# Layer 1's modulations of x summed on VectorE and GpSimd during the products with w_out

## The chip, the cores and the metric

The kernel runs on one core of a Trainium2 chip. The engines work side by side, each through its own queue of instructions in a fixed order: TensorE (PE in the profile, with its weight loads as PEld) multiplies matrices into PSUM, VectorE (DVE), ScalarE (ACT) and GpSimd (POOL) work element by element, and SyncE (SP) issues most of the DMAs between HBM and SBUF. The metric is the time of one execution on the device in microseconds (us), as the median of several runs. Lower is better.

## The reference

A diffusion transformer of two layers, with 512 image tokens (x) and 256 context tokens (ctx), width 1024. Each layer first makes modulations out of a conditioning vector: one product with w_ada (1024 x 6144) gives six vectors of 1024 values, for x from c and for ctx from c_ctx.

```python
def adaln(cond, w_ada, b_ada):
    m = jax.nn.silu(cond) @ w_ada + b_ada
    return jnp.split(m, 6, axis=-1)
...
    for l in range(DEPTH):
        update_ctx = l < DEPTH - 1
        sh1, sc1, gt1, sh2, sc2, gt2 = [m[:, None, :] for m in adaln(c, w_ada[l], b_ada[l])]
        csh1, csc1, cgt1, csh2, csc2, cgt2 = adaln(c_ctx, w_ada[l], b_ada[l])
        h = rms_norm(x, g_mix[l]) * (1 + sc1) + sh1
        hc = rms_norm(ctx, g_mix[l]) * (1 + csc1) + csh1
        ...
        x = x + gt1 * (o @ w_out[l])
        x = x + gt2 * swiglu(rms_norm(x, g_ffn[l]) * (1 + sc2) + sh2, w_gate[l], w_up[l], w_down[l])
        if update_ctx:
            ...
    return rms_norm(x, g_final)
```

Between the two lies a mixer: six heads of global attention, a Fourier mix and six heads of attention in a window. In layer 1 ctx is not updated any more, so that there only sh1 and sc1 of ctx are needed, and of the chunks 2 to 5 (gt1, sh2, sc2, gt2) only those of x.

## The kernel before

All data is kept transposed: 1024 channels as eight blocks of 128 partitions, the tokens along the free dimension. Most products are made in three matmuls from operands split into a high and a low part (`mm3`, L90; `split`, L103: ScalarE rounds the high part, VectorE subtracts for the low one).

The modulations come in three groups of two chunks each (`adaln`, L251). A step loads one block of 128 rows and 2048 columns of w_ada (1 MB, on SP, into one of the two `raw` staging buffers) and multiplies it on TensorE by a stationary block of 32 columns of `ct`, in which two columns hold silu(c) and silu(c_ctx): four matmuls side by side in four column strips of the array (L278). In the attention VectorE adds the result to a sum in SBUF (L290). After eight steps `last` transposes the sum back (L296), adds the bias (L301) and makes the scale with the norm's gain (`mod`, L313). So c and ctx are served at once.

Layer 0's group 0 is made at the start. All else is made in the second half of each layer's attention (the six window heads), as fill: `mix` (L1056) gives each piece of filling work a cost, and `attention` (L970) hands out pieces after each finished unit (two query blocks of one head, 12 units in layer 1) in proportion to the units done. The list `ada` has groups 1 and 2 of the layer itself and, in layer 0, group 0 of layer 1; it is interleaved with the steps of the Fourier mix. A step of `ada` costs 2.5, of `fb` (Fourier inputs) 5, of the Fourier mix 1.3.

`w_out` (L1165) then loads x back (`xt`, L1173), and goes through the eight output blocks d, two to a load (`load_pair`, L142, 1 MB, in `raw`). `one` makes the product of a block for a range of tokens in one of three PSUM banks (`mm`), and VectorE adds it to x (L1182); ScalarE squares it for the next norm (L411), VectorE sums the squares (L415). The first four blocks are made for all tokens (x: `XR`, then ctx: `CR`), the last four (`late`) first for x, so that its norm can begin (`stat`, L425 and L426, matmuls against a column of ones; `rstd`, L339 on GpSimd; L441), and only then for ctx. In layer 1 there is no ctx, and x is done in two halves. The norm's results (L1212 to L1222) feed the first product of the feed-forward part (`first`, L1362), while `tokens` (L1261) makes sums of token blocks into the tiles th0 to th3 and tl0 to tl3. `spare` (L1235) lends these same tiles for other uses before and after that time.

The order on each engine is not simply that of the code: a planner lays the instructions out by the readiness that it expects and by their place in the code, and adds the waits. The queue of an engine, SP's among them, is then in order: an instruction that waits holds up all behind it.

Of the kernel before, what the change touches and what calls it, by code (L numbers as in the profile page):

```python
# [11 lines left out]
AF = mybir.ActivationFunctionType  # L12
ALU = mybir.AluOpType
# [4 lines left out]
P = 128  # L18
D = 1024
KB = D // P  # L20
# [26 lines left out]
class Builder:  # L47
# [68 lines left out]
    def raw(self):  # L116
        return self.wp.tile([P, 2048], F32, name=self.nm("raw"), tag="raw", bufs=2)
# [133 lines left out]
    def adaln(self, l, g, raw, psum, tile, hold=KB, js=range(4)):  # L251


        nc = self.nc
        n = len(js)
        dj = js[1] - js[0]
        jv = slice(js[0], js[-1] + 1, dj)
        w = self.a["w_ada"][l].rearrange("k (g j c) -> k g j c", j=4, c=512)[:, g, jv]
        st = {}

        by = 4 // n
        e = 32 * n * by

        def step(k0):


            if k0 % hold == 0:
                st["ps"] = psum()
            rs = []
            for k in range(k0, k0 + by):  # L270
                rs.append(raw()[:, 0 : n * 512].rearrange("p (j c) -> p j c", c=512))
                self.queue(rs[-1], w[k * P : (k + 1) * P])
            end = None
            for i in reversed(range(by)):
                with self.tc.issue_after(end) if end else ExitStack():
                    for j in range(n):
                        o = 32 * (n * i + j)
                        end = nc.tensor.matmul(  # L278
                            st["ps"][o : o + 32, :],
                            self.ct[:, k0 + i, :],  # L280
                            rs[i][:, j],
                            start=(k0 % hold == 0),
                            stop=((k0 + by) % hold == 0),
                            tile_position=(0, o),
                        ).ins
            if k0 + by == hold:
                st["sb"] = tile()[0:e, 0:512]
                nc.scalar.copy(st["sb"], st["ps"][0:e])
            elif (k0 + by) % hold == 0:
                nc.vector.tensor_add(st["sb"], st["sb"], st["ps"][0:e])  # L290

        def last():
            sb = st["sb"]
            pt = psum() if hold < KB else st["ps"]
            for cb in range(4):
                nc.tensor.transpose(pt[:, cb * e : (cb + 1) * e], sb[:, cb * P : (cb + 1) * P], self.ident[0:e, 0:e])  # L296
            gj = lambda v: v.rearrange("p (g j c) s -> p g j c s", g=3, c=4)[:, g, jv]
            src = pt[:, 0 : 4 * e].rearrange("p (c i j s) -> p i j c s", c=4, i=by, s=32)[:, :, :, :, 0:2]
            b = gj(self.bada[l].unsqueeze(2)).to_broadcast([P, n, 4, 2])
            for i in range(by):  # L300
                nc.vector.tensor_tensor(gj(self.ada[l]), src[:, i], gj(self.ada[l]) if i else b, op=ALU.add)  # L301
            for i in range(2):
                ks = [4 * (4 * g + j - (24 * i + 8) // 4) for j in js]
                ks = [k for k in ks if 0 <= k < KB]
                if ks:
                    self.mod(l, i, slice(ks[0], ks[-1] + 4))

        return [lambda k=k: step(k) for k in range(0, KB, by)] + [last]

    def mod(self, l, i, r):  # L310
        g = (self.gmix if i == 0 else self.gffn)[l][:, r]
        sc = self.ada[l][:, 24 * i + 8 : 24 * i + 16, :][:, r]
        self.nc.vector.scalar_tensor_tensor(  # L313
            self.smod[l][i][:, r], sc, 1.0, g.unsqueeze(2).to_broadcast([P, r.stop - r.start, 2]), op0=ALU.add, op1=ALU.mult
        )
# [740 lines left out]
    def mix(self, l, hi, lo, ws, outs):  # L1056
        nc = self.nc
        full = l < DEPTH - 1
        self.qkv_tiles(full)
        krs, rms, turn = self.qkv_a(l, hi, lo, ws, outs)  # L1060
# [33 lines left out]
        for f in va:  # L1094
# [3 lines left out]
        mods = lambda m, g: cost(  # L1098
            2.5, self.adaln(m, g, self.raw, self.fl, lambda: self.f2([P, 512], "sb"), 1)
        )  # L1100
# [3 lines left out]
            for c, tb in ((kc, 3), (qc, 2)):  # L1104
                c[0] = (0, lambda f=c[0][1], tb=tb: self.late(f, tb))
        fill = kc[0:3] + qc[0:1] + kc[3:] + qc[1:]
        ada = mods(l, 1) + mods(l, 2)
        if full:
            ada += mods(l + 1, 0)

        held = []

# [52 lines left out]
    def w_out(self, l, oh, ol):  # L1165

        nc = self.nc
        full = l < DEPTH - 1
        w = self.a["w_out"][l]
# [4 lines left out]
        acc = self.fp.tile([P, T], F32, name=self.nm("acc"), tag="acc", bufs=1)  # L1174
        hs = [self.utile(F32) for k in range(KB)]

        def one(d, wt, rng, s):
            r0, r1 = rng
            ps = self.mm()[:, 0 : r1 - r0]
            wh, wl = wt  # L1180
            self.mm3(ps, [(wh[:, k], wl[:, k], oh[k][:, r0:r1], ol[k][:, r0:r1]) for k in range(KB)])
            nc.vector.scalar_tensor_tensor(  # L1182
                xt[d][:, r0:r1], ps, self.gt(l, 0, d, s), xt[d][:, r0:r1], op0=ALU.mult, op1=ALU.add
            )
            self.stat_add(acc, xt[d], rng, d)

        rngs = (XR,) if full else XH
        late = []
        for dp in range(KB // 2):
            rv = self.load_pair(w[:, dp * 256 : (dp + 1) * 256])  # L1190
            for j in range(2):
                d = 2 * dp + j
                wt = self.pair_half(rv, j)
                if d >= KB - LATE:
                    late.append((d, wt))
                    continue
                one(d, wt, XR, 0)
                if full:
                    one(d, wt, CR, 1)
        bcs = []  # L1200
        for rng, bank in zip(rngs, (self.fl, self.mm)):
            for d, wt in late:
                one(d, wt, rng, 0)
            bcs.append(self.stat_bc(acc, rng, bank()))
        hi, lo = self.act
        n = (T if full else SX) // 2
        last = []
# [24 lines left out]
                self.norm_raw(hs[k], xt[k], bc, CR, l, k, 1)  # L1232
        return xt, hs

    def spare(self, i):  # L1235

        tag = ("th", "tl")[i // 4] + str(i % 4)
        t = self.fp.tile([P, 3, T // 2], F32, name=self.nm("sp"), tag=tag, bufs=1)
        return t.rearrange("p a b -> p (a b)")[:, 0:512]

    def utile(self, dt):
        return self.fp.tile([P, T], dt, name=self.nm("u"), tag="u", bufs=8)
# [642 lines left out]
```

## Time and profile before

| | |
|---|---|
| time of three runs | 1558.27 us median (1555.56 to 1558.91) |
| profiled execution | 1555.41 us, of it 1553.6 us of span |
| mean granted TensorE clock | 0.99 |
| VectorE, ScalarE, GpSimd busy | 73%, 49%, 36% of the span |
| loads of w_ada | 40 of 1 MB in the attention of both layers, 16 of 512 KB at the start |

The span is the time from the first to the last instruction. In the profile a line L278 is line 278 of the kernel before; a helper's line stands for all who call it, so groups are told apart by tiles (`fl<-raw,ct` is a matmul into PSUM tile fl from raw and ct). A number behind x is a count of instructions, then come the busy time, the mean duration in ns and the idle time of the engine just before, with what ended it.

### The profile page before, as it was taken

The numbers are of one execution on the slowest core, as the hardware profiler recorded it, in microseconds if no ns is written. First come the engines' busy times: TensorE is split into PE (matmuls) and PEld (weight loads), VectorE is DVE, ScalarE is ACT, GpSimd is POOL, SyncE is SP. The second block draws the span as 40 slices with busy tenths as digits, with TensorE's granted clock in tenths as the row PEclk, the third lists the DMA queues.
The fourth block names the chain that finished last, engine by engine and source line by source line (L and its number), as shares of the span: only waits on it lengthen the run. The fifth ranks groups of instructions, "written<-read, shape, count | busy, mean of one in ns | idle before, by whom it ended". The sixth has DMA issues, their size and how long they took to land.

```text
span 1553.6 us, 25611 instructions
## 1 busy us (share of the span) xinstructions
PE 1485.4 (96%) x9769; PEld 1363.6 (88%) x9769; DVE 1133.1 (73%) x1907; ACT 763.9 (49%) x1542; POOL 556.7 (36%) x463
## 2 busy tenths in 40 slices
PE   6989989999999999999999998999999999999997
PEld 3789967688999999999899978987799898988987
DVE  3767577753978878876887866667749778777775
ACT  3556566642744444444435545666637344444344
POOL 0354345310256656452000025353401444344432
PEclk9999999999999999999999999999999999999999
DMA  9510085851133543446883541065441423223221
GB/s 339 197 48 29 1 263 159 290 190 29 54 130 130 163 138 123 161 137 227 307 301 110 167 128 35 28 201 189 141 134 52 136 82 109 83 82 126 92 82 55
DMA packets 124298, 211.59 MB, mean 136 GB/s; under 512 B 6456, under 2 KB 87120, under 8 KB 119056
## 3 DMA queue, kind: packets, MB, share of 16 engines
q1 hardware_dynamic: 116320, 203.92, 38.2%
q0 software_dynamic: 7856, 6.04, 2.0%
q8 instruction: 77, 1.26, 0.3%
q14 instruction: 45, 0.37, 0.1%
HBM read 180.96 MB, written 28.97 MB: 135 GB/s over the span
## 4 chain that ended last, share of the span: by engine, by line
PE 69%; DVE 10%; DMA 8%; ACT 4%; POOL 4%; issue 4%; SPq 1%; POOLq 0%; DVEq 0%; ACTq 0%
PE mm L90 15%; PE lg L90 14%; PE fl L90 13%; DVE w L103 5%; PE mm L1506 4%; PE mm L945 4%; PE lg L1506 4%; PE mm L937 2%; ACT w L103 2%; PE fl L278 2%; DMA raw<-in_w_up_dram 2%; PE lg L833 2%; PE lg L841 2%; DMA ra<-in_w_ada_dram 2%; PE fl L1506 1%
## 5 line engine op out<-in xcount | busy, mean ns | idle before, releaser
L103 DVE TENSOR_TENSOR w<-raw,w 128x512 fp32r<-128x512 f32 (+1 forms) x336 | 314.7, 949 | 113.5 <-ACT w L103 108.1
L103 ACT CAST w<-raw 128x512 fp32r<-128x512 f32 (+1 forms) x336 | 228.5, 701 | 316.4 <-POOL raw L1324 94.1
L90 PE MATMUL lg<-ahi,w 128*128 128x384 f32 (+1 forms) x640 | 151.2, 312 | 6.9 <-DVE w L103 3.1
L90 PE MATMUL fl<-ahi,w 128*128 128x384 f32 (+1 forms) x640 | 153.5, 308 | 0.9 <-ACT acc L1385 0.9
L852 POOL TENSOR_TENSOR p<-p,rc 128x768 f32<-128x768 f32 (+2 forms) x84 | 111.4, 1344 | 116.9 <-DVE rc L850 105.3
L90 PE MATMUL lg<-th,w 128*128 128x384 f32 (+1 forms) x640 | 150.4, 311 | 1.4 <-DVE u L1448 1.2
L90 PE MATMUL mm<-u,w 128*128 128x512 f32 (+1 forms) x576 | 137.9, 378 | 3.9 <-DVE u L103 2.2
L339 POOL TENSOR_TENSOR rs<-ms,mhalf 128x8 f32<-128x8 f32 (+3 forms) x22 | 28.6, 1304 | 288.7 <-DVE ms L335 288.7
L90 PEld LDWEIGHTS lg<-ahi,w 128*128 128x128 f32 x640 | 111.5, 191 | 11.2 <-ACT w L103 5.1
L90 PE MATMUL fl<-w,ahi 128*128 128x256 f32 x576 | 115.0, 293 | 5.9 <-DVE w L103 3.8
L90 PEld LDWEIGHTS mm<-u,w 128*128 128x128 f32 x576 | 98.0, 190 | 20.9 <-DVE u L103 3.5
L90 PEld LDWEIGHTS lg<-th,w 128*128 128x128 f32 x640 | 111.7, 191 | 3.3 <-DVE u L1448 1.5
L90 PEld LDWEIGHTS fl<-ahi,w 128*128 128x128 f32 x640 | 112.0, 190 | 2.5 <-ACT acc L1385 1.1
L90 PE MATMUL mm<-ahi,w 128*128 128x256 f32 (+1 forms) x448 | 107.1, 330 | 0.0
L1324 POOL TENSOR_TENSOR raw<-raw 128x512 f32<-128x512 f32 x40 | 62.3, 1559 | 110.8 <-DVE w L103 110.8
L90 PEld LDWEIGHTS fl<-w,ahi 128*128 128x128 f32 x576 | 93.5, 196 | 8.0 <-DVE w L103 4.3
L103 DVE TENSOR_TENSOR t<-mm,t 128x512 fp32r<-128x512 f32 x108 | 74.0, 687 | 34.7 <-ACT t L103 34.0
L90 PE MATMUL lg<-tl,w 128*128 128x384 f32 (+1 forms) x320 | 99.3, 310 | 0.0
L90 PE MATMUL lg<-alo,w 128*128 128x384 f32 (+1 forms) x320 | 99.2, 310 | 0.0
L1316 POOL TENSOR_TENSOR s<-raw 128x512 f32<-128x512 f32 x40 | 54.6, 1366 | 123.3 <-DMA raw<-in_w_up_dram 75.8
L90 PE MATMUL fl<-alo,w 128*128 128x384 f32 (+1 forms) x320 | 98.7, 308 | 0.0
L844 DVE TENSOR_REDUCE neg<-lg 128x1 f32<-128x768 f32 (+2 forms) x96 | 80.7, 851 | 19.9 <-PE lg L841 19.0
(367 smaller groups left out, 3980.7 us busy)
## 6 DMA issues: line engine op xcount, KB each, us to landing
raw<-in_w_ada_dram SPq DMA_DIRECT2D x40, 1024.0 KB, 4.9
raw<-in_w_gate_dram SPq DMA_DIRECT2D x22, 1024.0 KB, 5.2
raw<-in_w_up_dram SPq DMA_DIRECT2D x22, 1024.0 KB, 5.3
uh<-uh SPq DMA_DIRECT2D x33, 384.0 KB, 4.8
w<-uh SPq DMA_DIRECT2D x33, 384.0 KB, 4.6
wd<-in_w_down_dram SPq DMA_DIRECT2D x47, 256.0 KB, 5.1
raw<-in_w_in_dram SPq DMA_DIRECT2D x11, 1024.0 KB, 5.5
raw<-in_w_down_dram SPq DMA_DIRECT2D x11, 1024.0 KB, 4.8
```

The lines of the kernel that those rows point to most:

```text
L90: mm = lambda a, b, **k: self.nc.tensor.matmul(out, a, b, skip_group_check=more, **k)
L103: return self.nc.scalar.copy(hi, src).ins, self.nc.vector.tensor_sub(lo, src, hi).ins
L278: end = nc.tensor.matmul(st["ps"][o : o + 32, :], self.ct[:, k0 + i, :], rs[i][:, j], start=(k0 % hold == 0), stop=((k0 + by) % hold == 0) ...
L833: nc.tensor.matmul(o, qt[:, qs], K1[:, kv, k0 : k0 + w], start=True, stop=False)
L841: nc.tensor.matmul(o, qt[:, qs], K2[:, kv, k0 : k0 + w], start=False, stop=True)
L844: nc.vector.tensor_reduce(ng, lv, axis=AX.X, op=ALU.max, negate=True)
L852: nc.gpsimd.tensor_tensor(pt, pt, rc[:, i : i + 1].to_broadcast(list(pt.shape)), op=ALU.mult)
L937: nc.tensor.transpose(ps[:, col + j * P : col + (j + 1) * P], pt[:, c : c + P], self.ident)
L945: nc.tensor.matmul(out[:, r], V[:, kb, kv, :], t[:, c], start=first and n == 0, stop=end and n == len(todo) - 1,)
L1316: nc.gpsimd.tensor_add(s1, a21, a22)
L1324: nc.gpsimd.tensor_sub(a12, a12, a11)
L1506: nc.tensor.matmul(ps, w[:, x, c], u[:, y], start=(not more and k == 0 and j == 0), stop=(k == npc - 1 and j == 2), skip_group_check=True,)
```

## The change

Layer 1's groups 1 and 2 are not made in its attention any more: its list `ada` is empty, and layer 0's is as before. A new function `matvec` makes one chunk of 1024 values for x alone. A step loads 128 rows of w_ada and the chunk's 1024 columns (512 KB), and multiplies each row with its value of silu(c), a scalar for each partition, while adding it to a sum of 128 x 1024 in SBUF. The first step of a chunk writes the sum on ScalarE. The others are one instruction of VectorE, or, for a chunk with `pooled` set, a scaling on ScalarE and an addition on GpSimd. `last` adds up the 128 partitions: eight matmuls with a 128x128 block of the sum as the stationary operand and the column of ones as the moving one, into one bank; VectorE adds the bias and, for chunk 4, makes the scale.

Layer 0's `w_out` makes chunks 2 and 3 of layer 1 (VectorE; they share four buffers, and have one sum each) and chunk 4 (`pooled`, one buffer and one sum). Layer 1's `w_out` makes chunk 5 of its own (VectorE, the same four buffers). The buffers and sums are the tiles that `spare` lends, which now hands out 1024 columns where asked. The steps stand in the code after the products of `w_out`: after each call of `one` for the first four blocks, and for the late ones of x, `more` hands out a share of them, 27 in ten calls in layer 0 (every third one of chunk 4) and 9 in six calls in layer 1.

```diff
+    def matvec(self, l, i, room, acc, pooled):
+        nc = self.nc
+        w = self.a["w_ada"][l][:, i * D : (i + 1) * D]
+        st = {}
+
+        def step(k):
+            r = room()
+            nc.sync.dma_start(r, w[k * P : (k + 1) * P])
+            c = self.ct[:, k, 0:1]
+            if k == 0:
+                st["acc"] = acc()
+                nc.scalar.activation(st["acc"], r, AF.Identity, scale=c)
+            elif pooled:
+                nc.scalar.activation(r, r, AF.Identity, scale=c)
+                nc.gpsimd.tensor_add(st["acc"], st["acc"], r)
+            else:
+                nc.vector.scalar_tensor_tensor(st["acc"], r, c, st["acc"], op0=ALU.mult, op1=ALU.add)
+
+        def last():
+            ps = self.lg1()[:, 0:KB]
+            for k in range(KB):
+                nc.tensor.matmul(ps[:, k : k + 1], st["acc"][:, k * P : (k + 1) * P], self.ones, start=True, stop=True)
+            r = slice(i * KB, (i + 1) * KB)
+            a = self.ada[l][:, r, 0]
+            nc.vector.tensor_tensor(a, ps, self.bada[l][:, r], op=ALU.add)
+            if i == 4:
+                nc.vector.scalar_tensor_tensor(self.smod[l][1][:, :, 0], a, 1.0, self.gffn[l], op0=ALU.add, op1=ALU.mult)
+
+        return [lambda k=k: step(k) for k in range(KB)] + [last]
...
-        ada = mods(l, 1) + mods(l, 2)
-        if full:
-            ada += mods(l + 1, 0)
+        ada = mods(l, 1) + mods(l, 2) + mods(l + 1, 0) if full else []
...
+        turn = [0, 4, 1, 5]
+
+        def room():
+            i = turn.pop(0)
+            turn.append(i)
+            return self.spare(i, 1024)
+
+        if full:
+            one3 = self.matvec(l + 1, 2, room, lambda: self.spare(2, 1024), False)
+            two3 = self.matvec(l + 1, 3, room, lambda: self.spare(3, 1024), False)
+            own = self.matvec(l + 1, 4, lambda: self.spare(6, 1024), lambda: self.spare(7, 1024), True)
+            mods = []
+            for i, f in enumerate(one3 + two3):
+                mods.append(f)
+                if i % 2:
+                    mods.append(own.pop(0))
+            every = len(mods) / 10
+        else:
+            mods = self.matvec(l, 5, room, lambda: self.spare(2, 1024), False)
+            every = len(mods) / 6
+        made = [-every]
+
+        def more():
+            made[0] += every
+            while mods and made[0] > 0.5:
+                made[0] -= 1
+                mods.pop(0)()
+
         for dp in range(KB // 2):
...
                 one(d, wt, XR, 0)
+                more()
                 if full:
                     one(d, wt, CR, 1)
+                    more()
         bcs = []
         for rng, bank in zip(rngs, (self.fl, self.mm)):
             for d, wt in late:
                 one(d, wt, rng, 0)
+                more()
             bcs.append(self.stat_bc(acc, rng, bank()))
...
-    def spare(self, i):
+    def spare(self, i, w=512):
...
-        return t.rearrange("p a b -> p (a b)")[:, 0:512]
+        return t.rearrange("p a b -> p (a b)")[:, 0:w]
```

## The prediction

> **What bounds the kernel now.** I read the page first: busy time and share of the span of each engine.
>
> ```profile
> PE 1485.4 (96%) x9769; PEld 1363.6 (88%) x9769; DVE 1133.1 (73%) x1907; ACT 763.9 (49%) x1542; POOL 556.7 (36%) x463
> ```
>
> TensorE is busy for 96% of the span. That is an average, so next comes the view of busy time by stretches, over the places that the change touches: layer 0's w_out (337 to 395), the start of its feed-forward part (395 to 432), the second half of layer 1's attention (1027 to 1130), and layer 1's w_out (1130 to 1165).
>
> ```profile
> core 0: us, PE busy (x) PEld busy (x) DVE busy (x) ACT busy (x) POOL busy (x), PEclk, DMA share, GB/s
> 337.00:385.00 48.00, 48.00 (x267) 41.98 (x266) 18.10 (x26) 10.92 (x17) 0.00 (x0) 1.00 0.28 97
> 385.00:395.00 10.00, 10.00 (x88) 10.00 (x87) 6.80 (x11) 4.53 (x8) 1.03 (x1) 1.00 0.34 107
> 395.00:432.00 37.00, 36.67 (x219) 36.59 (x218) 36.88 (x70) 27.81 (x58) 8.01 (x6) 1.00 0.09 29
> 1027.00:1060.00 33.00, 31.34 (x243) 23.04 (x243) 25.57 (x42) 20.17 (x41) 14.72 (x13) 1.00 0.79 271
> 1060.00:1102.00 42.00, 42.00 (x333) 34.91 (x335) 32.22 (x62) 27.05 (x65) 17.97 (x16) 1.00 0.46 164
> 1102.00:1130.00 28.00, 24.66 (x156) 19.97 (x150) 18.68 (x33) 15.75 (x35) 9.05 (x7) 0.94 0.49 167
> 1130.00:1165.00 35.00, 35.00 (x230) 32.16 (x229) 16.53 (x26) 10.98 (x17) 3.44 (x2) 1.00 0.34 110
> ```
>
> Columns: the stretch, its length, each engine's busy time (instructions). TensorE is the bound in every one of them. In layer 0's w_out VectorE has 29.9 us free of 48, ScalarE 37, and GpSimd did nothing. From 395 to 432 VectorE is as full as TensorE (36.88 and 36.67 of 37): no room there. From 1102 to 1130, the tail of layer 1's attention, TensorE is idle for 3.3 us.
>
> **What is removed.** Layer 1's two lists of modulation steps (groups 1 and 2) leave its attention. The groups of lines have their matmuls (between 1027 and 1107) and their additions on VectorE (all lists); below them three pieces of the chain in order of time (start, length, what).
>
> ```profile
> L278 PE MATMUL fl<-raw,ct 128*32 128x512 f32 x128 | 18.1, 604 | 1.3 <-issue 1.0 <-DMA raw<-in_w_ada_dram 0.2
> ...
> L290 DVE TENSOR_TENSOR sb<-sb,fl 128x512 f32<-128x512 f32 x35 | 23.9, 683 | 9.2 <-PE fl L278 8.8
> ```
>
> ```profile
> 1037.97 1.00 PE fl L278 x8
> ...
> 1059.89 0.44 PE fl L296 x4
> ...
> 1102.97 5.18 DMA raw<-in_w_out_dram
> ```
>
> 128 records in eights are 16 steps. The busy 18.1 us count ends that overlap with other matmuls; on the chain a step takes 1.00 us, so 16.0 in all. The four transposes that close a list take 0.44 us, for two lists 0.9. TensorE's waits in front of the steps, 1.0 + 0.2 = 1.2 us, go too. Together **-18.1 us**, if TensorE stays the bound. What is late next: between 1027 and 1102 TensorE is left with 73.3 - 15 x 1.00 = 58 us of work, VectorE with 57.8 less some 13 additions of 0.68, so 49, ScalarE with 46. TensorE still leads, by 18%.
>
> The fill between the heads is dealt out by cost. Without the steps (18 at a cost of 2.5) its total falls from 68 to 23, so the rest of the fill comes later and closer: the first Fourier step after about half of the heads instead of after two of twelve. Its work is the same and still ends with the last head; I cost that at nothing, between -1 (fewer clashes) and +3 (the idle time that TensorE shows in the tail, again).
>
> The sixteen loads of 1 MB go as well. They hold the two staging buffers that w_out's weights need (the third row above). The last step releases the buffer, and then 5.2 us pass until w_out's first weights land, with their splits in the attention's tail on ScalarE and VectorE. The load will now be issued early. The gain lies between 0 and the 3.3 us that TensorE idles there; the other waiters of that tail (softmax and its splits) stay, so I take a bit under half, **-1.5 us**.
>
> **What is added.** Four vectors (chunks 2, 3, 4 in layer 0's w_out, chunk 5 in layer 1's) of eight loads of 512 KB and one closing step each. The closing step has eight matmuls against a column of ones. The same form, stationary 128x128 with one moving column, stands in the norm's sums:
>
> ```profile
> 385.62 0.36 PE L425 MATMUL mm<-ones,acc 128*128 128x1 f32 x2
> ...
> 386.73 0.36 PE L426 MATMUL mm<-ones,sq 128*128 128x1 f32 x2
> ```
>
> Five of those pairs take 386.73 - 385.62 = 1.11 us, 0.222 each. 4 x 8 x 0.222 = 7.1 us on TensorE, in stretches without a gap: **+7.1 us** (5.3 in layer 0, 1.8 in layer 1).
>
> The products of weights and vector have the nearest rows in the groups of lines by shape:
>
> ```profile
> L103 DVE TENSOR_TENSOR w<-raw,w 128x1024 fp32r<-128x1024 f32 x64 | 81.6, 1278 | 16.7 <-ACT w L103 11.7 <-PE lg L90 3.5 <-DMA xt<-xsc 0.5
> ...
> L103 ACT CAST w<-raw 128x1024 fp32r<-128x1024 f32 x64 | 67.0, 1052 | 43.0 <-PE mm L90 25.7 <-PE lg L90 10.3 <-DMA raw<-in_w_in_dram 2.8
> ...
> L711 POOL TENSOR_TENSOR qcx<-t,t 128x512 f32<-128x512 f32 x4 | 5.2, 1294 | 12.8 <-DVE t L710 12.8
> ```
>
> VectorE takes 1.28 us for 128x1024 with two inputs, ScalarE 1.05, GpSimd 2.6 (twice its half). In layer 0, VectorE has 14 such products, 18 us in 29.9 free ones; ScalarE 10, 10.5 us in 37; GpSimd 7, 18.2 us, where it was idle. TensorE waits for VectorE only when the three product banks are full, and today VectorE waits for TensorE:
>
> ```profile
> 376.18 0.75 DVE L1182 SCALAR_TENSOR_TENSOR xt<-mm,ada,xt 128x512 f32<-128x512 f32 x1 [2.90 <-PE mm L90]
> ```
>
> So these lie beside other work, as long as they end before 395. Whether they do is set by their loads and by the chain on GpSimd:
>
> ```profile
> GB/s 339 197 48 29 1 263 159 290 190 29 54 130 130 163 138 123 161 137 227 307 301 110 167 128 35 28 201 189 141 134 52 136 82 109 83 82 126 92 82 55
> ...
> ra<-in_w_ada_dram SPq DMA_DIRECT2D x16, 512.0 KB, 9.7
> ...
> raw<-in_w_in_dram SPq DMA_DIRECT2D x4, 512.0 KB, 5.0
> ```
>
> ```profile
> 331.59 5.76 SPq L1173 DMA_DIRECT2D xt<-xsc  x8
> ```
>
> ```profile
> 420.28 0.54 DVE L103 TENSOR_TENSOR tl<-u,th 128x384 fp32r<-128x384 f32 x1
> ```
>
> The loads queue on SP behind x (issued until 337.4). 24 of them are 12.6 MB; with 2 MB of w_gate and w_up, at the 339 GB/s of the busiest slice, 43 us: until about 380. The two vectors on VectorE have four buffers and end by then. Chunk 4 has one buffer, so its load, scaling and addition follow one another: with the 5.0 us landing 8 x 5.0 + 8 x 1.05 + 7 x 2.6 = 67 us, so 404; with five loads in flight 5 x 0.52 MB / 339 GB/s = 7.7 us (the 9.7 of the first rows is such a burst), for all eight 88 us, so 425. The first steps are crowded and the last ones alone: I take 414. Its buffers are wanted back by the first tl splits at about 420, and chunk 4 itself only in layer 1, so being late costs nothing by itself. Behind each waiting load on SP stand w_gate and w_up, which the feed-forward part needs shortly before 395; they wait for one load at a time, so some 10 us, and have twice that. If that cover went, each microsecond would be one on TensorE.
>
> Two things are not hidden. GpSimd's short instruction for the norm's root, on the way to the feed-forward part, can stand behind one 2.6 us addition. And two engines can stop each other, as the timelines of GpSimd and VectorE show:
>
> ```profile
> 399.31 1.60 POOL L1317 TENSOR_TENSOR raw<-raw 128x512 f32<-128x512 f32 x1
> ```
>
> ```profile
> 396.21 0.61 DVE L1217 SCALAR_TENSOR_TENSOR alo<-u,ada,ahi 128x384 fp32r<-128x384 f32 x1
> ...
> 399.70 1.62 DVE L1217 SCALAR_TENSOR_TENSOR alo<-u,ada,ahi 128x384 fp32r<-128x384 f32 x1
> ```
>
> A VectorE instruction that takes 0.61 us alone took 1.62 beside a GpSimd addition, ending 0.41 us after it. Two or three additions fall after 395, where VectorE is full. For both, and for TensorE meeting the ones matmuls a little early, I take **+3.0 us**, one addition with its hand-over; the ends are 0 and the second rival's 16. In layer 1's w_out seven products of 1.28 us on VectorE (16.5 of 35 busy) and no GpSimd addition: nothing.
>
> Sum: -18.1 - 1.5 + 7.1 + 3.0 = **-9.5 us**. The profiled execution took 1555.4 us, 1553.6 of span and 1.8 around it, so 1545.9; the median of the runs is 2.9 above it: **1549 us**.
>
> The Trainium skill (SBUF — State Buffer, "SBUF: two separate sides") speaks against the change: it states that VectorE with two SBUF inputs and GpSimd take one pair of ports as an exclusive lock for a whole instruction. The 1.62 us row agrees with it. By that rule all seven additions could stop VectorE, and the sum would be the third rival's or worse; without it, mine or the last rival's.
>
> **The rivals.**
> - *Attention doesn't shrink in full* (0.12). Without the fill, the path from logits over VectorE, ScalarE and GpSimd back to TensorE could set the pace. For it: VectorE would be at 49 of 58 us, and the tail shows such idle time. Against: from 1060 to 1102 TensorE has no gap. At half of 18.1: -0.4, 1558.
> - *TensorE held by GpSimd's chain* (0.14), the other side. TensorE works in a fixed order, and chunk 4's ones matmuls stand where the planner thinks them ready; behind them stand w_out's last products. The chain is 8 links long, so an error in each adds up. Placed at 404 and ready at 420, between the two ends: 16 us instead of my 3, so +3.5, 1562. It decides from a wait of some 12 us on. In code order, behind the third of the late tiles (the L1182 row at 376.18), even the 404 would mean a wait of 27, so 1573. Against: the order is not that of the code, since the first product of w_out runs ahead of attention's last ones,
>
> ```profile
> 324.96 0.50 PE L90 MATMUL mm<-ahi,w 128*128 128x512 f32 x1
> ...
> 329.98 0.39 PE L945 MATMUL mm<-t,Vc 128*128 128x256 f32 x2
> ```
>
> and waits for planned loads are small (0.2 us in the 16 steps above).
> - *VectorE stopped by GpSimd* (0.14). Three additions after 395 stop a full VectorE for 3 x 2.6 = 7.8 us, and TensorE follows: -4.7, 1553.
> - *Better* (0.10): no stall, the tail's idle time gone: -18.1 - 3.3 + 7.1 = -14.3, 1544.
>
> My own case has 0.50. About 0.2% (3.1 us) can be told from no change. Faster by more: 0.50 + 0.14 + 0.10 = 0.74; within: the first rival, 0.12; slower: 0.14. The range runs from 1541 to 1560: it takes in all but the GpSimd chain's own cases and some hundredths below.
>
> **What would show it.** Right: in layer 1's attention no L278 and L296, and the time from its second half's start to w_out's is some 19 us shorter with TensorE still full; the new ones matmuls in pairs at 0.22 us; VectorE with 21 products near 1.3 us, GpSimd with 7 additions near 2.6; TensorE's waits between 337 and 432 under 4 us. Wrong: TensorE idle in front of the ones matmuls of chunk 4 or of x's first feed-forward products, L1217 or the splits at twice their time, or gaps of over 5 us in layer 1's attention.

## The result, and where the time went

The changed kernel takes 1577.4 us (median of 4 runs, 1576.4 to 1581.7) beside 1557.0 for the kernel before (4 runs, 1555.6 to 1558.9): ratio 1.0136, 95% interval 1.0112 to 1.0159. It is **slower by about 20 us**, where 1549 us were forecast. The profiled execution has a span of 1576.3 us, 22.7 more than before (the execution profiled before, at 1555.4 us, was one of the shorter ones). The page's first part for the changed kernel, busy time and share of the span:

```profile
PE 1488.6 (94%) x9697; PEld 1376.1 (87%) x9697; DVE 1148.9 (73%) x1916; ACT 773.8 (49%) x1551; POOL 571.8 (36%) x470
```

TensorE has 72 matmul records fewer (9769 before: 136 of the lists went, 64 of the sums came) and yet 3.2 us more of busy time. The columns of a norm's sum take 0.36 us a pair at a granted clock of 1.00 and 0.57 at 0.50 (rows of this trace), so busy time alone doesn't tell work. Three marks in the timeline show where the span grew: the start of layer 1's last matmul in qkv_first, its first projection (line 522 before the change), of the last matmul with the sinks in layer 1's attention (828), and of the program's last transposes (1767). The table has each mark, and the two stretches between them, for the kernels that the text comes back to (us).

| kernel | mark 522 | against before | 522 to 828 | against before | 828 to 1767 |
|---|---|---|---|---|---|
| before | 921.4 | | 191.1 | | 433.1 |
| changed | 951.6 | +30.2 | 185.1 | -6.0 | 431.6 |
| attention_alone | 923.0 | +1.6 | 181.9 | -9.2 | 431.9 |
| bank_fl | 935.6 | +14.2 | 184.6 | -6.5 | 429.4 |
| chunk4_vector | 929.7 | +8.3 | 182.7 | -8.4 | 430.1 |
| the same again | 932.1 | +10.7 | 185.5 | -5.6 | 431.1 |
| no_max | 930.6 | +9.2 | 173.5 | -17.6 | 433.8 |
| no_max_before | 922.7 | +1.3 | 188.7 | -2.4 | 431.8 |

Each row is one trace. The two of chunk4_vector are of one kernel, and are 2.4, 2.8 and 1.0 us apart: a difference of that size between two rows says nothing by itself.

So two things went other than forecast: layer 0 **lost 30 us** around its w_out, and layer 1's attention **gained 6 us** of the 18 that were removed from TensorE. Busy time by stretches of the changed kernel, the prediction's stretches (those of layer 1 moved by the 30 us):

```profile
core 0: us, PE busy (x) PEld busy (x) DVE busy (x) ACT busy (x) POOL busy (x), PEclk, DMA share, GB/s
337.00:385.00 48.00, 48.00 (x270) 42.02 (x269) 36.15 (x40) 17.00 (x22) 7.40 (x3) 1.00 0.85 309
385.00:395.00 10.00, 10.00 (x64) 10.00 (x62) 3.72 (x5) 2.51 (x3) 3.38 (x2) 0.66 0.19 55
395.00:432.00 37.00, 22.57 (x122) 21.51 (x121) 33.41 (x56) 26.40 (x48) 15.34 (x9) 0.68 0.31 100
1057.00:1090.00 33.00, 29.35 (x213) 27.25 (x211) 24.87 (x41) 23.57 (x47) 11.65 (x10) 0.95 0.25 65
1090.00:1132.00 42.00, 38.12 (x262) 34.62 (x261) 30.15 (x57) 27.40 (x66) 21.32 (x20) 0.92 0.00 1
```

Columns as before: length, busy time (instructions) by engine, granted clock. In the first row all is as forecast: TensorE is full, and VectorE took up its products (36.15 us busy, 18.10 before). In the third, TensorE is busy for 22.57 of 37 us and at 0.68 of its clock. The 30.2 us come together, within that scatter, from: 14.1 us more idle (14.4 against 0.3); clock lost in the third row, 22.57 x 0.32 = 7.2; clock lost in the second row, 10.00 x 0.34 = 3.4; and the ones matmuls of three chunks, 5.3. Sum 30.0. In the last two rows TensorE idles for 3.65 and 3.88 us, where before it was 1.66 and 0.

The idle time on TensorE, from its timeline (start, length, what, in brackets the idle time before it and what ended it):

```profile
401.30 0.28 PE L90 MATMUL mm<-ahi,w 128*128 128x256 f32 x1
408.97 0.58 PE L457 MATMUL mm<-ones,acc 128*128 128x1 f32 x2 [7.39 <-DVE acc L447]
...
415.80 1.23 PE L473 MATMUL mm<-ident,rs 128*128 128x128 f32 x4 [4.96 <-POOL rs L371]
418.93 1.01 PE L1442 MATMUL mm<-ahi,w 128*128 128x384 f32 x2 [1.91 <-ACT ahi L103]
...
420.89 3.41 PE L333 MATMUL lg<-ones,sp 128*128 128x1 f32 x16
424.15 0.67 PE L1442 MATMUL lg<-ahi,w 128*128 128x384 f32 x1
```

The waits carry the names of VectorE and GpSimd, but the last two rows hold the cause. Before, x's first feed-forward products into tag lg started at 395.6 and filled this stretch while the norm of the context rows was made (timeline of TensorE, kernel before):

```profile
395.60 0.51 PE L1380 MATMUL lg<-ahi,w 128*128 128x384 f32 x2
```

Now they stand behind L333, chunk 4's ones matmuls, which wait for its sum. TensorE works through what stands ahead of them, the context path, and that comes one wait after the other. Tag lg has two buffers, handed out in the order of the code: to chunk 2, chunk 3, chunk 4, and then to the two tiles of x's first products, of which one needs chunk 4's buffer. The sum was as late as the prediction thought possible (timeline of GpSimd, first and last of the seven additions):

```profile
361.38 2.65 POOL L326 TENSOR_TENSOR sp<-sp,sp 128x1024 f32<-128x1024 f32 x1 [26.20 <-issue]
...
418.17 2.37 POOL L326 TENSOR_TENSOR sp<-sp,sp 128x1024 f32<-128x1024 f32 x1
```

It ends at 420.5; the prediction had 404 to 425 and took 414.

### The profile page after: what moved, and what is told of

It is laid out like the page before. It is cut to its first block, busy times and chain, and to the rows that moved or that the text cites. A ratio compares the mean times of both kernels' runs of the same rounds, so it can differ in the third digit from the quotient of the medians.

```text
span 1576.3 us, 25513 instructions
## 1 busy us (share of the span) xinstructions
PE 1488.6 (94%) x9697; PEld 1376.1 (87%) x9697; DVE 1148.9 (73%) x1916; ACT 773.8 (49%) x1551; POOL 571.8 (36%) x470
## 4 chain that ended last, share of the span: by engine, by line
PE 64%; DVE 11%; DMA 8%; POOL 6%; ACT 5%; issue 4%; SPq 0%; POOLq 0%; DVEq 0%; ACTq 0%
PE mm L90 14%; PE fl L90 12%; PE lg L90 11%; DVE w L103 5%; PE mm L1568 4%; PE lg L1568 3%; PE mm L977 3%; DMA raw<-in_w_up_dram 3%; PE mm L969 2%; ACT w L103 2%; PE lg L865 1%; PE fl L278 1%; POOL raw L1386 1%; PE lg L873 1%; PE fl L1568 1%
## 5 line engine op out<-in xcount | busy, mean ns | idle before, releaser
L103 DVE TENSOR_TENSOR w<-raw,w 128x512 fp32r<-128x512 f32 (+1 forms) x336 | 305.9, 923 | 132.3 <-ACT w L103 127.1
L90 PE MATMUL mm<-ahi,w 128*128 128x256 f32 (+1 forms) x448 | 111.0, 338 | 0.0
```

Of the source, the lines that this page charges most:

```text
L90: mm = lambda a, b, **k: self.nc.tensor.matmul(out, a, b, skip_group_check=more, **k)
L103: return self.nc.scalar.copy(hi, src).ins, self.nc.vector.tensor_sub(lo, src, hi).ins
```

## The experiments

**The two parts by themselves.** attention_alone leaves the sums out, so that these modulations hold the bias alone (bias copies it):

```diff
-        return [lambda k=k: step(k) for k in range(KB)] + [last]
+        return [lambda: None] * KB + [bias]
```

> The changed kernel without the four vectors' loads, products and ones matmuls: chunks 2 to 5 of layer 1's modulations hold the bias alone. It measures what layer 1's attention gains without its modulation steps. Theory A (TensorE stays the bound there, as the prediction had it): 18 to 20 us below the kernel before, about 1538. Theory B (without the steps as fill, logits and softmax wait for each other and the granted clock sinks in the gaps): 7 to 9 us below, about 1549, with the windows from 1040 to 1110 showing TensorE idle for 1.5 to 2.5 us in each 20 and a granted clock of 0.83 to 0.93 in them, as in the changed kernel.

1549.2 us against 1557.6 (9 and 24 runs), ratio 0.9948 (0.9933 to 0.9964): 8.4 us less. That is theory B's time; the 18 to 20 us of theory A are not there. The idle time of theory B is there too (2.1 us in each of the two stretches from 1060 shown below), its clock only in part: 0.91 from 1040 to 1060, then 1.00.

sums_alone keeps the lists as well:

```diff
-        ada = mods(l, 1) + mods(l, 2) + mods(l + 1, 0) if full else []
+        ada = mods(l, 1) + mods(l, 2)
+        if full:
+            ada += mods(l + 1, 0)
```

> The four vectors are summed as in the changed kernel, and layer 1's attention keeps its modulation steps as well, so the work is done twice with the same values. It measures what the sums cost alone. Theory A (the prediction's terms: 7.1 for the ones matmuls, 3.0 for stalls): 10 us above the kernel before. Theory B (TensorE stands before chunk 4's ones matmuls and the first feed-forward products behind them): 29 to 33 us above before, nearly all of it between 337 and 432. If the two parts add up, this and attention_alone sum to the change's +20.

1584.6 us, ratio 1.0176 (1.0149 to 1.0203): 27 us more, a little under B's 29 to 33 and far from A's 10. Together the parts give 27 - 8 = +19, the change's own +20.

**What holds TensorE in layer 0.** bank_fl leaves the sum on GpSimd as it is and moves its closing step behind the norm and out of tag lg:

```diff
-            ps = self.lg1()[:, 0:KB]
+            ps = (self.fl() if pooled else self.lg1())[:, 0:KB]
...
+            end4 = mods.pop()
...
                 self.norm_raw(hs[k], xt[k], bc, CR, l, k, 1)
+            end4()
```

> The changed kernel with chunk 4's closing step moved in the code behind the norm of the feed-forward part's first rows and its ones matmuls put into PSUM tag fl in place of lg; the sum on GpSimd stays as it is. Theory A (the hold-up is the two lg banks, which the first feed-forward products need and chunk 4 keeps until its sum is there): TensorE's gap in 400 to 420 closes, and the time is 15 to 20 us below the changed kernel, about 1558 to 1562. Theory B (the hold-up is the load on VectorE and GpSimd themselves, shared ports and late norms): at most 5 us below, about 1573 to 1577.

1561.9 us, ratio to before 1.0025 (1.0011 to 1.0039): 15.5 us below the changed kernel, as theory A has it. Its busy time by stretches, and the last of its GpSimd additions:

```profile
395.00:432.00 37.00, 33.74 (x199) 32.46 (x198) 29.53 (x51) 24.43 (x44) 15.46 (x9) 0.91 0.32 100
```

```profile
421.22 2.84 POOL L326 TENSOR_TENSOR sp<-sp,sp 128x1024 f32<-128x1024 f32 x1
```

The sum ends at 424.1, 3.5 us later than in the changed kernel, yet TensorE is busy for 33.74 us in place of 22.57. So the late sum by itself cost little, and what its closing held cost most of the time. The edit moves the closing in the order and to another tag at once; which of the two frees TensorE was not separated.

chunk4_vector takes chunk 4 off GpSimd and leaves its closing where it was:

```diff
-        turn = [0, 4, 1, 5]
+        turn = [0, 4, 1, 5, 6] if full else [0, 4, 1, 5]
...
-            own = self.matvec(l + 1, 4, lambda: self.spare(6, 1024), lambda: self.spare(7, 1024), True)
+            own = self.matvec(l + 1, 4, room, lambda: self.spare(7, 1024), False)
```

> The changed kernel with chunk 4 summed on VectorE like the others, with one buffer more in their turn, and closed through lg as in the changed kernel; GpSimd makes no additions there. Theory A (the late GpSimd sum is what holds the lg bank): layer 0 loses 5 to 12 us instead of 31, since 21 products of 1.28 us are 27 of VectorE's 30 free ones, and the time is 1552 to 1560. Theory B (any ones matmuls that stand in lg before the first feed-forward products hold TensorE): still 1570 or more.

> The same kernel as chunk4_vector, beside the two others on their chip: 2 to 5 us below before, about 1554.

1554.1 us, ratio 0.9980 (0.9965 to 0.9994), and the second time 1554.7, 0.9985 (0.9972 to 0.9998): 23 us below the changed kernel and **3 us below before**. Theory A: a closing in lg doesn't hold TensorE up if its sum is there in time. VectorE bore it, by its instructions and the same stretch:

```profile
L328 DVE SCALAR_TENSOR_TENSOR sp<-sp,ct,sp x28: 1274/1279/1286, 350.8 to 1156.3; 128x1024 f32<-128x1024 f32 x28
```

```profile
395.00:432.00 37.00, 37.00 (x233) 37.00 (x232) 33.17 (x64) 25.44 (x50) 7.63 (x6) 0.95 0.10 33
```

28 products of 1279 ns, none stretched, and TensorE without a gap.

bank_fl still takes 7.8 us more than chunk4_vector. Ahead of mark 522 it has lost 14.2 us, against 8.3 and 10.7 in the two traces of chunk4_vector, and from 395 to 432 its TensorE idles for 3.26 us where chunk4_vector's doesn't. GpSimd's additions remain there: they stand before the norm's root in its queue and stop VectorE (last section). The runs don't share the difference out between the two.

**Why the attention gains half.** Half of the change, chunks 2 and 3 alone, with chunks 4 and 5 left in the attention:

```diff
+        ada = mods(l, 2)
+        if full:
+            ada = mods(l, 1) + ada + mods(l + 1, 0)
...
+            mods = one3 + two3
...
+            mods = []
```

> Half of the change: only chunks 2 and 3 are summed on VectorE in layer 0's w_out; chunks 4 and 5 stay as modulation steps in layer 1's attention, and nothing is summed in layer 1's w_out or on GpSimd. Eight steps leave the attention (8.0 us, 0.4 for one closing) and 3.6 us of ones matmuls come. Theory A (the first steps that leave are worth their full time, since eight remain as fill): 3 to 5 us below before, about 1553. Theory B (each step is worth the same half of its time, as 8.5 of 18 in attention_alone): 4.2 - 3.6, so within 1 us of before, 1557.

1559.5 us, ratio 1.0013 (1.0000 to 1.0027): 2 us more, worse than both theories. By the marks eight steps less (8.4 us by their own time) shorten the stretch from 522 to 828 by 2.3 us only, so the first steps to leave are not worth their full time. Ahead of mark 522 this trace has lost 7.4 us (928.8), with 3.6 us of ones matmuls in it; where the rest went was not followed.

Is it where the rest of the fill lies? In the changed kernel the six Fourier steps ran early, up to about 1085, and the heads after them had none. fourier_spread ties each behind the last product of the head ahead of it in the code (behind does that):

```diff
-        ada = mods(l, 1) + mods(l, 2) + mods(l + 1, 0) if full else []
+        ada = mods(l, 1) + mods(l, 2) + mods(l + 1, 0) if full else cost(2.5, [lambda: None] * 18)
...
+            for i in (2, 3, 5, 6, 7, 8):
+                four[i] = (four[i][0], lambda f=four[i][1]: self.behind(f))
```

> chunk4_vector with the six Fourier steps of layer 1's attention on TensorE each tied behind the last product of the head that stands before it in the code, and with the old steps' shares of the fill kept as empty entries, so that the Fourier steps lie in the second half of the heads and not bunched ahead of 1060. Theory A (the attention gains too little because the fill is used up early and the later heads have none): 4 to 10 us below chunk4_vector, 1544 to 1550, with fewer waits for p in the last 40 us. Theory B (without the modulation steps there is too little fill in all, wherever it lies; the heads' own path over ScalarE, VectorE and GpSimd sets the pace): within 2 us of chunk4_vector's 1554.

1557.2 us, ratio 1.0001 (0.9990 to 1.0012), 3 us above chunk4_vector. By the marks the stretch from 522 to 828 is 2.0 us shorter than in chunk4_vector and the rest 4.0 longer (4.8 and 3.0 beside its second trace): at most, time moved from one to the other. The place of the fill isn't what costs the time. Theory A falls, and the time lies 1 us outside theory B's band as well, on the slow side.

Is it a PSUM bank? third_bank_fl relieves tag lg, which the logits and each head's third bank share (quick is set for layer 1's second half):

```diff
-            ps = self.lg1() if bi == 2 else self.mm()
+            ps = (self.fl if self.third else self.lg1)() if bi == 2 else self.mm()
...
-            filler(whole * done / total)
+            filler(whole * done / total * (2 if self.quick else 1))
+            self.third = self.quick and not fill
```

> chunk4_vector with two edits in layer 1's second half of the attention: the fill (bias projection and Fourier steps) is dealt out in the first half of the heads, and from then on the third bank of each head's products comes from tag fl, which the modulation steps used before, and not from lg, whose two buffers also take the logits. Theory A (TensorE's waits for p and for lg are the two lg buffers, of which each head takes three turns): 3 to 6 us below chunk4_vector, with the waits for p, 5.1 us there, at half. Theory B (the heads' path over VectorE, ScalarE and GpSimd is itself the limit, whatever bank it goes through): within 1.5 us of chunk4_vector.

1556.2 us, ratio 0.9997 (0.9987 to 1.0007), and chunk4_vector beside it 1554.7: no gain, theory B. The waits for p behind L860 fall from 3.2 to 2.5 us between 1060 and 1115, not to half. The run also deals the fill out earlier, so a small gain from the bank could hide behind a loss from that.

Then it is the way of a head itself. no_max is chunk4_vector with that way shortened: it leaves the maximum out and takes the exponential of 0.01 of the logits, in layer 1's second half of the attention (the edit there). TensorE's work is the same:

```diff
-            nc.vector.tensor_reduce(ng, lv, axis=AX.X, op=ALU.max, negate=True)
-            nc.scalar.activation(pt, lv, AF.Exp, bias=ng, accum_out=den[:, i : i + 1])
+            nc.scalar.activation(pt, lv, AF.Exp, scale=0.01, accum_out=den[:, i : i + 1])
```

> chunk4_vector with a shorter path for the twelve units of layer 1's second half of the attention: the maximum over the logits (VectorE, 0.75 us a row, two rows a unit) is left out, and the exponential takes 0.01 of the logits so that it stays finite. TensorE's work is unchanged. Theory A (without the modulation steps the round trip of a head, logits to maximum to exponential and back to the lg buffer, sets the pace): 4 to 9 us below chunk4_vector, 1546 to 1551, with TensorE's idle time from 1040 to 1120 at half of the 8 us there. Theory B (TensorE's own work sets the pace and its waits are chance): within 1.5 us of chunk4_vector.

1545.9 us against 1557.3 (6 and 17 runs), ratio 0.9918 (0.9900 to 0.9937): 8 us below chunk4_vector. no_max_before is the same edit in the kernel before.

> The kernel before with the same part left out (no maximum, the exponential of 0.01 of the logits, in layer 1's second half of the attention). Theory A: the modulation steps cover the round trip there, so shortening it is worth little, 0 to 3 us below before. If it is worth as much as in no_max, the steps covered nothing, and theory A is wrong.

1557.2 us, ratio 0.9994 (0.9981 to 1.0008): nothing. Busy time by stretches over the same 40 us of four kernels, first before, then attention_alone, no_max, no_max_before:

```profile
1060.00:1080.00 20.00, 20.00 (x154) 16.08 (x153) 13.71 (x27) 12.07 (x30) 7.70 (x7) 1.00 0.37 132
1080.00:1100.00 20.00, 20.00 (x162) 17.00 (x161) 16.54 (x33) 13.52 (x32) 9.63 (x9) 1.00 0.60 212
```

```profile
1060.00:1080.00 20.00, 17.89 (x133) 16.06 (x133) 15.80 (x32) 14.47 (x36) 10.84 (x11) 1.00 0.00 1
1080.00:1100.00 20.00, 17.98 (x132) 15.89 (x131) 15.15 (x29) 13.61 (x33) 11.15 (x11) 1.00 0.00 1
```

```profile
1060.00:1080.00 20.00, 19.09 (x150) 18.35 (x149) 11.28 (x25) 16.28 (x41) 11.75 (x11) 1.00 0.04 13
1080.00:1100.00 20.00, 19.38 (x163) 19.03 (x163) 11.60 (x25) 16.54 (x41) 12.08 (x11) 1.00 0.00 1
```

```profile
1060.00:1080.00 20.00, 19.93 (x153) 15.85 (x151) 8.91 (x20) 12.05 (x29) 8.29 (x8) 1.00 0.46 166
1080.00:1100.00 20.00, 20.00 (x161) 16.83 (x159) 11.85 (x24) 13.31 (x32) 9.08 (x9) 1.00 0.61 199
```

Without the steps TensorE idles for 2 us of each 20 in both stretches, while VectorE is at 79% and 76% and ScalarE at 72% and 68%: no engine is full. With a shorter way of a head the idle time falls to 0.9 and 0.6. With the steps it is 0.1 at most, with or without the maximum. What TensorE waits for says the same (the view of waits, chunk4_vector and then no_max, 1060 to 1115; us in all, times, longest):

```profile
PE lg L860 <- ACT p L877: 3.2, 8, 0.5
PE mm L977 <- ACT t L103: 1.4, 5, 0.4
```

```profile
PE lg L860 <- ACT p L877: 1.7, 4, 0.6
```

The logits of a head wait for an lg buffer until ScalarE has taken the exponential of an earlier row: logits, maximum, exponential, and round again. In the kernel before, the modulation steps ran in that time: about half of what they took lay in a gap. The profiled executions of chunk4_vector and no_max are 4.7 us apart (spans of 1550.6 and 1545.9), and TensorE's idle time between the marks 522 and 828 is 4.1 of it. Leaving the maximum out also takes 17.9 us off VectorE between 1060 and 1115 (24 rows of 0.75), so the shorter way and the emptier VectorE are not told apart; that VectorE was idle for about a fifth of the time speaks for the way.

**The ones matmuls and the clock.** In the second row of the stretches above TensorE is never idle, yet the clock is 0.66. Two kernels add to the kernel before 24 one-column matmuls that nothing reads, in one burst ahead of the norm's eight (shown), or in four bursts of six behind the first four products for the context rows:

```diff
+            if full and not bcs:
+                ps = self.fl()
+                with self.after(self.last):
+                    for c in range(24):
+                        nc.tensor.matmul(ps[:, c : c + 1], self.ident, self.ones, start=True, stop=True)
             bcs.append(self.stat_bc(acc, rng, bank()))
```

> The kernel before with 24 more one-column matmuls (stationary ident, moving ones, as many as the change adds in layer 0) in one burst on TensorE right before the norm's own eight in layer 0's w_out; nothing reads them. By their own time (24 x 0.222) 5.3 us above before. If a run of one-column matmuls lets the granted clock sink though TensorE never idles: 9 to 13 above, with a granted clock near 0.5 in the 5 to 10 us behind the start of the burst.

> The kernel before with the same 24 one-column matmuls in four bursts of six, each behind a product of layer 0's w_out with 256 columns. Both theories: 5 to 6 us above before, with the granted clock at 1.00 from 337 to 400. If this costs as much as columns_together, the clock isn't what the burst costs.

Together 1565.4 us, ratio 1.0049 (1.0036 to 1.0062); apart 1561.1, 1.0018 (1.0007 to 1.0028): 7.9 and 3.5 us. Both lie below what was expected, since 5.3 us of columns cost only 3.5, but the difference of 4 us is there, and the stretches show it (the burst starts at 381.9; first the one, then the other kernel):

```profile
382.00:384.00 2.00, 2.00 (x21) 2.00 (x19) 0.75 (x1) 0.63 (x1) 0.00 (x0) 1.00 0.00 0
384.00:386.00 2.00, 2.00 (x18) 2.00 (x17) 0.00 (x0) 0.00 (x0) 0.00 (x0) 0.89 0.00 0
386.00:388.00 2.00, 2.00 (x12) 2.00 (x11) 0.00 (x0) 0.00 (x0) 0.00 (x0) 0.50 0.00 0
...
394.00:396.00 2.00, 2.00 (x12) 2.00 (x12) 0.00 (x0) 0.00 (x0) 0.00 (x0) 0.55 0.00 0
396.00:398.00 2.00, 2.00 (x19) 2.00 (x19) 0.67 (x2) 1.26 (x2) 0.00 (x0) 1.00 0.00 0
```

```profile
380.00:400.00 20.00, 20.00 (x135) 18.40 (x134) 7.34 (x12) 4.28 (x7) 1.03 (x1) 1.00 0.18 54
```

Ten microseconds near half clock, 5 us lost, with TensorE busy throughout. third_and_closing_fl puts this to use: it is third_bank_fl with chunk 4's closing behind the norm as in bank_fl, so that no closing stands next to another.

> third_bank_fl with chunk 4's closing step behind the norm of the context rows and in tag fl, as in bank_fl, so that the closings of layer 0 stand as three bursts of eight and none stands next to another. If the burst of 25 records at 396 in chunk4_vector costs its half clock (399 to 403) and nothing else: 1 to 3 us below third_bank_fl, with a granted clock of 1.00 from 380 to 420. If the late closing takes as much from the feed-forward part: within 1 us.

1553.9 us, ratio 0.9978 (0.9970 to 0.9987): 2.3 below third_bank_fl, and the clock is 1.00 from 380 to 440 where third_bank_fl has 0.94 and 0.89 (380 to 400, 400 to 420). Beside chunk4_vector, 1554.1 and 1554.7, it is no further step that these runs can tell. Both beat both kernels of this study, by 3 to 4 us against before.

## Why the prediction failed, step by step

- **"-18.1 us, if TensorE stays the bound": this step failed.** It was tested by "58 us of work, VectorE with ... 49, ScalarE with 46. TensorE still leads, by 18%". These are sums of busy time. But a head goes from engine to engine with two lg buffers, and its round trip, not any engine's sum, is what is late next. Measured between the marks: -5.6 to -9.2 us in the five traces without the steps and with the maximum (changed kernel, attention_alone, bank_fl, chunk4_vector twice). Where it went shows the whole stretch in the kernel before and in the two traces of chunk4_vector:

```profile
921.40:1112.50 191.10, 179.98 (x1382) 158.12 (x1380) 136.71 (x253) 116.65 (x239) 90.76 (x76) 0.98 0.36 118
```

```profile
929.70:1112.40 182.70, 166.08 (x1245) 156.20 (x1244) 130.84 (x239) 117.52 (x239) 92.31 (x78) 0.97 0.14 38
```

```profile
932.10:1117.60 185.50, 168.42 (x1245) 158.75 (x1244) 130.90 (x239) 117.36 (x239) 92.34 (x78) 0.95 0.13 37
```

TensorE's busy time falls by 13.9 and 11.6 us and its idle time grows from 11.1 to 16.6 and 17.1. That growth is the largest part of what the step had wrong. The difference between the two traces of one kernel is mostly busy time at a lower clock. The first rival had the mechanism and even the half, at 0.12. no_max, with the round trip shortened, has -17.6; that this comes so near to 18.1 is chance, with traces 3 us apart.
- **The fill's order, cost "at nothing, between -1 and +3": the reason didn't hold, the cost was not contradicted.** The prediction had the Fourier steps come late; they came early. With them late, fourier_spread took 3 us more, not less.
- **"being late costs nothing by itself", and +3.0 for stalls: this step failed**, and it cost most. The chain ended at 420.5, within the bounds given; who would want its sum was answered with "only in layer 1". But the closing step stands in TensorE's fixed order and takes an lg buffer that x's first feed-forward products need next. In the place of 3 stood 14.1 of idle time and 7.2 of clock lost after it. The second rival had the wait, TensorE held in front of these ones matmuls, and its size, 16 us. It put w_out's last products behind them, but those ran (until 401.6), and the feed-forward part's first stood there; and it left out the clock.
- **w_out's weights early, -1.5: not contradicted, not measured.** From mark 828 on, the changed kernel took 1.5 us less with 1.8 us of ones matmuls in it, and attention_alone, which has none there, 1.2 less. Both agree with the step, but two traces of one kernel differ by 1.0 there.
- **Ones matmuls, 4 x 8 x 0.222 = 7.1: their own time was right** at full clock (1.84 us for chunk 3's eight), and the burst's effect on the clock was missing, 3.4 us in layer 0. In columns_apart 24 of them cost 3.5 us of the whole kernel (1.1 to 4.4), less than their 5.3; why was not looked into.
- **The products' durations and cover: right.** VectorE 1277 ns (1.28), GpSimd 2438 (2.6), ScalarE 1144 (1.05); until 395 they lay beside TensorE's work.
- **VectorE stopped by GpSimd, the third rival: it happened**, by at least five of the seven additions (last section), twice in the stretch in which TensorE stood. What it added to that wait was not separated.
- **The range** took each rival with all else as forecast. The first and the second came together: 1549 + 9 + 13 = 1571 by the prediction's own prices, outside 1541 to 1560. They don't exclude each other, and nothing in the prediction said why one of them should come alone.

## What to carry to other kernels

Taking away work that fills a gap gains only what it takes beyond the gap, not its busy time: before an instruction stream is taken off the bound engine, ask what that engine would do in its place, and measure the round trip of what remains (logits, maximum, exponential, buffer), not the sums of the engines. A result that nobody needs for a long time can still hold a buffer or a place in an engine's order; for everything moved, look up which PSUM tag its last step takes and who takes that tag next. And rivals that have separate mechanisms must be added up too, not only listed one beside the other.

## What the hardware showed that was not expected

**Matmuls of one column let the clock sink while TensorE is busy.** In the changed kernel chunk 3's closing stands right before the norm's sums (timeline of TensorE, then busy time by stretches):

```profile
384.89 1.84 PE L333 MATMUL lg<-ones,sp 128*128 128x1 f32 x16
...
388.50 0.57 PE L458 MATMUL mm<-ones,sq 128*128 128x1 f32 x2
```

```profile
384.00:386.00 2.00, 2.00 (x20) 2.00 (x19) 0.00 (x0) 0.01 (x1) 0.89 (x1) 1.00 0.11 12
386.00:388.00 2.00, 2.00 (x17) 2.00 (x16) 0.17 (x1) 0.00 (x0) 0.00 (x0) 0.83 0.81 256
388.00:390.00 2.00, 2.00 (x10) 2.00 (x11) 0.16 (x1) 1.15 (x1) 0.66 (x1) 0.50 0.01 2
...
394.00:396.00 2.00, 2.00 (x18) 2.00 (x18) 0.88 (x3) 0.25 (x1) 0.00 (x0) 0.96 0.38 76
```

4.0 us of one-column matmuls, from 384.89 to 388.93, and the clock is at half from about 387.4 to 394. The kernel before has the norm's part of that run alone, 1.5 us (385.48 to 386.96), and a clock of 1.00 there. Chunk 2's closing, alone at 372.4, left the clock at 1.00 too. The Trainium skill (TensorE: Matmul & The Clock Gate, "Part 1: The HAM clock gate (the "warmup" mystery)") states that the clock goes to half after an idle window of about 3.4 us and comes back after a busy one. The lengths here agree with such windows; but TensorE had no idle time in them, so one-column matmuls seem to count for little as activity. What in their form makes it so was not tried.

**GpSimd stopped VectorE for whole instructions.** VectorE's timeline beside four of the seven additions (361.38, 390.36, 401.79 and 409.09):

```profile
361.69 2.62 DVE L447 TENSOR_TENSOR acc<-acc,sq 128x256 f32<-128x256 f32 x1
...
391.24 2.57 DVE L103 TENSOR_TENSOR w<-raw,w 128x1024 fp32r<-128x1024 f32 x1 [0.38 <-ACT w L103]
...
402.68 2.54 DVE L103 TENSOR_TENSOR w<-raw,w 128x1024 fp32r<-128x1024 f32 x1 [1.37 <-ACT w L103]
...
410.17 1.92 DVE L1279 SCALAR_TENSOR_TENSOR alo<-u,ada,ahi 128x384 fp32r<-128x384 f32 x1
```

Alone these take 0.41, 1.22, 1.22 and 0.60 us in the same trace; together they lost 6.2 us, and each ended 0.3 to 1.1 us behind the addition beside it. A fifth addition, at 372.54, stretched a product of 1.28 us to 1.63. Beside the one at 382.49 VectorE had only an instruction that reads PSUM (L1212), and it kept its 0.75 us. The Trainium skill (SBUF — State Buffer, "SBUF: two separate sides") states that VectorE with two SBUF inputs and a GpSimd instruction that reads SBUF take a pair of ports as an exclusive lock, and that whichever starts first has it for its whole instruction. The trace agrees with it: in each case GpSimd's addition had started first.

**The granted clock sank among gaps of half a microsecond.** In layer 1's attention of the changed kernel no single wait is longer than 0.7 us, and the clock from 1090 to 1132 is 0.92, with 38.12 of 42 us busy. attention_alone, with the same kind of waits, had 1.00 from 1060 to 1120. Nor does the kernel alone decide: the two traces of chunk4_vector, in the same 20 us, have 1.00 and 0.83, with the same busy time of TensorE (the second is some 2.7 us behind the first in its work).

```profile
1060.00:1080.00 20.00, 17.56 (x129) 15.80 (x128) 16.50 (x30) 14.78 (x35) 10.29 (x9) 1.00 0.01 2
```

```profile
1060.00:1080.00 20.00, 17.56 (x110) 16.23 (x110) 14.00 (x26) 12.17 (x28) 8.05 (x7) 0.83 0.13 43
```

What does decide it was not tried.
